# Query and key norms of eight attention heads, in two layouts: channel by token, and token by channel group

## The chip, the core and the metric

The kernel runs on one core of a Trainium2 chip: TensorE (PE) multiplies, VectorE (DVE), ScalarE (ACT) and GpSimd (POOL) work elementwise, SyncE (SP) issues most transfers. The metric is the device time of one execution in microseconds.

## The reference

One inference step of a layer: 512 prompt frames and 64 sample frames, width 2048, all in fp32. Only the attention heads matter here:

```python
def rmsnorm(x, g):
    xf = x.astype(jnp.float32)
    y = xf * lax.rsqrt(jnp.mean(xf * xf, axis=-1, keepdims=True) + EPS) * g.astype(jnp.float32)
    return y.astype(x.dtype)
...
hn = rmsnorm(x, g_norm1)
proj = hn @ w_in
q, k, v, gb, gc, hc = jnp.split(proj, ...)
q = rmsnorm(q.reshape(B, T, N_HEADS, HEAD_DIM), g_q)
k = rmsnorm(k.reshape(B, T, N_HEADS, HEAD_DIM), g_k)
v = v.reshape(B, T, N_HEADS, HEAD_DIM)
o_attn = stick_breaking_blocks(q, k_all, v_all, P).reshape(B, T, ATTN_W)
```

q and k are normed per frame and head, over 128 channels; the normed keys are an output. `EPS` is 1e-6. A convolution branch, an output projection and a gated feed-forward follow.

## The kernel before, in words

Data stands as channels on 128 partitions by 576 frames (512 and 64), in two halves of 288. Products of full precision take three PE matmuls in fp32r, with operands split into a high and a low part (`split`: a ScalarE copy makes the high part, a VectorE subtraction the low one). The weights of one projection of one head (2048 x 128) come in by SP, into one of two places of `raw_a`, and are split in two pieces of 1024 columns, by ScalarE (`whi`) and VectorE (`wlo`, once POOL).

The input's own row norm is not applied to x ahead of the projection; it is a factor per frame, R1, which `row_scale` spreads to all partitions with PE and by which the projections' results are multiplied.

The heads run one after the other. `head(h)` projects q, k and v (`project`: 2 halves of 16 channel blocks, 3 matmuls each); after each channel block the `Pipeline` ticks. Everything else of a head is a generator that sleeps for a number of ticks between its steps, so its matmuls stand at fixed places among the projections', and attention of head h runs while head h+1 projects. The order on PE is the order of the program; on ScalarE, VectorE and POOL a scheduler orders the instructions ahead of time, and each engine then takes them strictly in that order. SP's order is written out from head 1 on.

`norm_evac` (lines 619 to 644) handles q and k. When a half of the projection is done, VectorE multiplies it by R1 into `E`, ScalarE squares it, and the square is split. Some ticks later (13 for q, 16 for k) `rest` sums over channels with two matmuls with a matrix of ones (`channel_sums`, tile `ss`), which puts the sum on every partition; `rsqrt_mean` makes a reciprocal root from it, with logarithm, exponential and one Newton step, all 288 wide; then the result times gain is written as `qf` or `kf` and split into `qh`, `ql`, `kh`, `kl`. Behind k's second half `attend` is started, 15 ticks on (24 in head 0).

`attend` (660 to 781) computes scores z in three banks of PSUM from those parts, and scores `zs` against cached keys; softplus steps on ScalarE and VectorE; a mask of later queries as a POOL product with a 0/1 matrix `m01`; running sums as matmuls with triangular matrices (`trir`, `trif`); then `po`, the weighted values of the prompt (from `vtok` and its parts `vh`, `vl`), `cz` and `os` for the samples. `kb` is the transposed k in 32 x 32 blocks, made by VectorE from `kf`, which `put_tokens` stores.

In head 0 q is projected while x still comes in; its banks wait (`defer`) until k has been projected and `row_scale` has run, and q's and k's four halves follow, 4 ticks apart.

`x_sums` makes combinations of x for a later stage during the heads; its transfers, copies and subtractions (`o_ob`, `xs_out`) sit in the same queues.

Of the kernel before, what the change touches and what calls it, by code (L numbers as in the profile page):

```python
# [16 lines left out]
P = 128  # L17
# [77 lines left out]
def tile_hybrid_stream_step(  # L95
# [23 lines left out]
    lpad = ctx.enter_context(tc.tile_pool(name="lpad", bufs=1, side="left"))  # L119
    lpad.tile([P, 8], F32, name="lpad_t")  # L120
    rpad = ctx.enter_context(tc.tile_pool(name="rpad", bufs=1, side="right"))
    rpad.tile([P, 56], F32, name="rpad_t")
    acon = tc.alloc_tile_pool(name="acon", bufs=1, side="left")
    xt_dram = tc.dram_tile([KD, P, T], F32, name="xt_dram")
    x2_dram = tc.dram_tile([KD, P, T], F32, name="x2_dram")
# [95 lines left out]
    def split(hi, lo, src, lo_eng=None):  # L221
        nc.scalar.copy(out=hi, in_=src)  # L222
        (lo_eng or nc.vector).tensor_tensor(out=lo, in0=src, in1=hi.bitcast(F32), op=ALU.subtract)  # L223

    def parts(name):
        t = tmp.tile([P, 2, HALF], F32R, tag="hl", name=name)
        return t[:, 0], t[:, 1]
# [15 lines left out]
                            pattern=[[-1, P]], channel_multiplier=1)  # L243
    trir = acon.tile([P, P], F32R, name="trir")
    nc.vector.tensor_copy(trir, trif)
    m01 = acA[:, 3, :]
    nc.gpsimd.affine_select(out=m01, in_=onef, compare_op=ALU.is_ge, fill=0.0, base=-1,
                            pattern=[[1, P]], channel_multiplier=-1)
    mneg = acA[:, 4, :]
    nc.vector.tensor_scalar(out=mneg, in0=m01, scalar1=-NEG, scalar2=NEG, op0=ALU.mult, op1=ALU.add)  # L250
    s01 = acA[:, 5, :TS]
    nc.gpsimd.affine_select(out=s01, in_=onef[:, :TS], compare_op=ALU.is_ge, fill=0.0, base=TS - 1,
                            pattern=[[1, TS]], channel_multiplier=-1)
    nc.gpsimd.memset(s01[:TS, :], 0.0)
    sneg = acA[:, 5, TS:]
    nc.vector.tensor_scalar(out=sneg, in0=s01, scalar1=-NEG, scalar2=NEG, op0=ALU.mult, op1=ALU.add)

    ps_z = tc.alloc_tile_pool(name="ps_z", bufs=1, space=PSUM)

    def misc(name):  # L260
        return ps_z.tile([P, 512], F32, tag="misc", name=name, bufs=2)
# [3 lines left out]
    def load_vectors():  # L265
        r0 = 0
        for name, ap, n in (("gq", g_q[0], 1), ("gk", g_k[0], 1),
                            ("ga", g_attn_out[0], NH), ("gc", g_conv_out[0], NG),
                            ("cw", conv_w[0].rearrange("w d -> (w d)"), 3 * NG),
                            ("st", state_conv[0, 0].rearrange("w d -> (w d)"), 2 * NG), ("g2", g_norm2[0], KD)):  # L270
            rows[name] = r0
            nc.sync.dma_start(out=vraw[r0 : r0 + n, :], in_=ap.rearrange("(r c) -> r c", c=P))
            r0 += n

    g1c = const.tile([P, KD], F32, name="g1c")
    vec = const.tile([P, P], F32, name="vec")
# [12 lines left out]
    def col(name, i=0):  # L289
        return vec[:, rows[name] + i : rows[name] + i + 1]  # L290
# [177 lines left out]
    def channel_sums(src_hi, src_lo, a, b, name):  # L468
        ps = misc(name)[:, : b - a]
        mm(ps, oner, src_hi, start=True, stop=False)  # L470
        mm(ps, oner, src_lo, start=False, stop=True)
        return ps
# [13 lines left out]
                                op0=ALU.mult)  # L486
    split_weight(nc.vector)

    def project(evac, banks=(None, None), defer=None, then=None):
        whi, wlo = next_weight()  # L490
        if then:
            then()
        for bank, (a, b) in zip(banks, HALVES):
            if bank:
                ps = ps_z.tile([P, 512], F32, tag=bank, name="pjz")[:, :HALF]
            else:
                ps = ps_pj.tile([P, HALF], F32, tag="pj", name="pj")
            product(ps, whi, wlo, slice(0, P), x_two, KD, a // HALF)
            if defer is None:
                evac(ps, a, b)  # L500
            else:
                defer.append((evac, ps, a, b))

    def add_squares(acc, src, first):
        if first:
# [108 lines left out]

    free_places = []

    lags = [0]

    def norm_evac(name, gcol, dst_f, dst_hi, dst_lo, first, after=None):
        E = t1.tile([P, T], F32, tag="E", name=f"E{name}", bufs=2)  # L620

        def rest(a, b, sh, sl):
            if first:
                lags[0] += 4
            yield 6 + lags[0] if first else 16 if after else 13
            ss = channel_sums(sh, sl, a, b, "ss")
            r = tmp.tile([P, HALF], F32, tag="r", name="r")
            rsqrt_mean(r, ss, P, HALF)
            nc.vector.scalar_tensor_tensor(out=dst_f[:, a:b], in0=E[:, a:b], scalar=gcol, in1=r,
                                           op0=ALU.mult, op1=ALU.mult)  # L630
# [12 lines left out]

        return evac

    def put_tokens(t, dst, a, b):

# [12 lines left out]
    def attend(h, st):  # L660
# [49 lines left out]
        nc.vector.transpose(out=kb, in_=kf)  # L710
        yield 8
        put_tokens(kb, kp[:, h, :], 0, TP)
        put_tokens(kb, ks[:, h, :], TP, T)

# [90 lines left out]
    def head(h):  # L805
        st = {}
        st["cK"] = t1.tile([P, TP], F32, tag="cK", name="cK")
        st["cV"] = t1.tile([P, 4, P], F32, tag="cV", name="cV", bufs=2)
        for q in range(4):
            nc.sync.dma_start(out=st["cK"][32 * q : 32 * (q + 1), :].rearrange("t (b c) -> t b c", c=32),  # L810
                              in_=ck[:, h, 32 * q : 32 * (q + 1)].rearrange("(b t) c -> t b c", t=32))
        nc.sync.dma_start(out=st["cV"], in_=cv[:, h, :].rearrange("(i p) d -> p i d", p=P))
        for n in ("q", "k"):
            st[n + "f"] = t1.tile([P, T], F32, tag=n + "f", name=n + "f")
            st[n + "h"] = t1.tile([P, TP], F32R, tag=n + "h", name=n + "h")
            st[n + "l"] = t1.tile([P, TP], F32R, tag=n + "l", name=n + "l")
        q_evac = norm_evac("q", gqs, st["qf"], st["qh"], st["ql"], h == 0)
        k_evac = norm_evac("k", col("gk"), st["kf"], st["kh"], st["kl"], h == 0, after=attend(h, st))
        pipe.spawn(keys_cached(st, 20 if h else 59))
        if h == 0:  # L820
            waiting = [(q_evac, ps, a, b) for ps, (a, b) in zip(q0ps, HALVES)]
            project(k_evac, (None, "z1"), waiting)
            row_scale()
            for evac, ps, a, b in waiting:
                evac(ps, a, b)
# [1039 lines left out]
```

## Time and profile before

| what | us |
|---|---|
| runs, median (lowest to highest of 3) | 2370.59 (2369.72 to 2371.94) |
| the profiled execution | 2369.07 |
| its span | 2367.0 |
| three steady heads, 165.77 to 309.15 | 143.38 |
| of it PE busy | 143.38 |
| of it VectorE busy | 110.93 |
| of it ScalarE busy | 88.78 |
| of it POOL busy | 20.45 |

In the timeline, each row has the start, the length, the engine, the line, the operation, output and inputs, and the shape; in brackets how long the engine sat idle ahead of it and what ended that. Matmuls overlap in the pipeline: a projection matmul is shown as some 0.29 us long, but the next one starts 0.13 us after it. What a matmul costs PE is the distance from start to start. A matmul in plain fp32 stands as two records, one per pass.

In the view by stretches, a row has the stretch, its length, and for PE, the weight loads, VectorE, ScalarE and POOL the busy time with the number of instructions, then the granted clock of PE, the busy share of the DMA engines and GB/s. In the list of waits a row has the waiting instruction, what it waited for, the total, the number of times and the longest.

### The profile page before, as it was taken

Reading aid. Unit: us, or ns where it says so; the run is one execution under the profiler, and the core shown is the slowest. Engines: PE = TensorE matmul, PEld = TensorE weight load, DVE = VectorE, ACT = ScalarE, POOL = GpSimd, SP = SyncE. Lnnn points to the kernel's source line nnn. Section 1 sums busy time; section 2 is a strip of 40 time slices with the busy share of each in tenths; the row PEclk is TensorE's granted clock in tenths of the full one; section 3 lists DMA queues with packets and bytes.
Section 4 is the critical chain, followed back from the end, with each engine's and each line's share of the span. In section 5 each row is a group of like instructions: output and inputs, shape, how many; then the busy total and the mean of one; then the engine's idle time right before and its main releaser. Section 6 shows DMA issues by size and latency. Waiting matters only on the chain.

```text
span 2367.0 us, 43888 instructions
## 1 busy us (share of the span) xinstructions
PE 2340.9 (99%) x17581; PEld 2329.5 (98%) x17581; DVE 1935.3 (82%) x2908; ACT 1156.0 (49%) x2039; POOL 294.5 (12%) x386
## 2 busy tenths in 40 slices
PE   8999999999999999999999999999999999999998
PEld 8999999999999999999999999999999999999998
DVE  7878777788887889888888888888888777887896
ACT  6656655444444555444444444444444444444443
POOL 1011111341111230000000000000000002431221
PEclk9999999999999999999999999999999999999999
DMA  8466544684368654444444444444444936885553
GB/s 259 128 175 169 139 138 112 217 266 126 110 226 227 194 166 154 137 152 136 139 152 135 140 152 134 141 152 133 142 152 132 356 115 208 221 235 199 190 143 85
DMA packets 588804, 395.74 MB, mean 167 GB/s; under 512 B 100030, under 2 KB 577720, under 8 KB 588600
## 3 DMA queue, kind: packets, MB, share of 16 engines
q1 hardware_dynamic: 574776, 375.93, 50.9%
q0 software_dynamic: 8624, 16.22, 3.4%
q8 instruction: 137, 2.24, 0.4%
q10 hardware_dynamic: 5200, 0.79, 0.2%
q14 instruction: 67, 0.55, 0.1%
HBM read 301.45 MB, written 91.44 MB: 166 GB/s over the span
## 4 chain that ended last, share of the span: by engine, by line
PE 89%; DVE 5%; DMA 2%; ACT 2%; issue 1%; POOL 0%; ACTq 0%; SPq 0%; POOLq 0%; DVEq 0%
PE psy L1532 33%; PE psw L1532 16%; PE pj L213 13%; PE psx L1532 8%; PE psy L1036 6%; PE pjo L213 4%; PE psw L1036 3%; PE psx L1036 2%; DVE whl L223 1%; DMA raw_a<-in_w_down_dram 1%; PE po L747 1%; PE z L679 1%; ACT whl L222 0%; PE os L777 0%; DVE whl L1008 0%
## 5 line engine op out<-in xcount | busy, mean ns | idle before, releaser
L1532 PE MATMUL psy<-h_s,whl 128*128 128x288 f32 x2787 | 411.7, 294 | 1.7 <-ACT part L1542 1.7
L213 PE MATMUL pj<-x,whi 128*128 128x288 f32 x1856 | 390.5, 297 | 0.3 <-DVE x L356 0.3
L1532 PEld LDWEIGHTS psy<-h_s,whl 128*128 128x128 f32 x2787 | 383.5, 188 | 2.6 <-ACT part L1542 2.6
L223 DVE TENSOR_TENSOR whl<-raw_a,whl 128x1024 fp32r<-128x1024 f32 (+4 forms) x296 | 318.3, 1076 | 57.3 <-ACT whl L222 55.6
L1532 PE MATMUL psw<-t,whl 128*128 128x288 f32 x2400 | 346.9, 294 | 0.0
L1532 PEld LDWEIGHTS psw<-t,whl 128*128 128x128 f32 x2400 | 327.6, 188 | 0.0
L222 ACT CAST whl<-raw_a 128x1024 fp32r<-128x1024 f32 (+4 forms) x296 | 267.6, 906 | 116.7 <-issue 35.3
L213 PEld LDWEIGHTS pj<-x,whi 128*128 128x128 f32 x1856 | 305.0, 189 | 1.0 <-DVE x L356 0.6
L213 PE MATMUL pj<-x,wlo 128*128 128x288 f32 x928 | 274.5, 296 | 0.1
L223 DVE TENSOR_TENSOR whl<-raw_b,whl 128x1024 fp32r<-128x1024 f32 (+5 forms) x190 | 198.1, 1042 | 68.6 <-ACT whl L222 67.2
L222 ACT CAST whl<-raw_b 128x1024 fp32r<-128x1024 f32 (+5 forms) x190 | 164.9, 871 | 169.6 <-issue 73.1
L1542 ACT COPY part<-psy 128x288 f32<-128x288 f32 x242 | 96.7, 400 | 281.9 <-PE psy L1532 258.4
L1532 PE MATMUL psy<-t2t,whl 128*128 128x288 f32 x1212 | 183.5, 295 | 1.2 <-ACT part L1542 1.2
L1532 PE MATMUL psy<-b22m,whl 128*128 128x288 f32 x1212 | 183.1, 295 | 0.6 <-ACT part L1542 0.6
L213 PEld LDWEIGHTS pj<-x,wlo 128*128 128x128 f32 x928 | 174.9, 188 | 0.7 <-DVE wlo L423 0.3
L1532 PE MATMUL psx<-h_s,whl 128*128 128x288 f32 x1185 | 173.7, 294 | 0.0
L1532 PEld LDWEIGHTS psy<-t2t,whl 128*128 128x128 f32 x1212 | 168.3, 188 | 1.6 <-ACT part L1542 1.4
L1532 PEld LDWEIGHTS psy<-b22m,whl 128*128 128x128 f32 x1212 | 168.1, 188 | 0.9 <-ACT part L1542 0.9
L1532 PEld LDWEIGHTS psx<-h_s,whl 128*128 128x128 f32 x1185 | 162.7, 188 | 0.0
L222 ACT CAST whl<-s 128x1024 fp32r<-128x1024 f32 (+5 forms) x81 | 72.2, 892 | 101.7 <-PE psw L1532 99.4
L1311 POOL DMA_DIRECT2D hid_dram<-form x3 | 2.3, 751 | 947.2 <-DVE form L223 947.2
L1532 PE MATMUL psy<-t,whl 128*128 128x288 f32 x576 | 106.5, 294 | 0.0
(456 smaller groups left out, 4392.5 us busy)
## 6 DMA issues: line engine op xcount, KB each, us to landing
hid_dram<-form SPq DMA_DIRECT2D x147, 288.0 KB, 2.3
raw_a<-in_w_in_dram SPq DMA_DIRECT2D x41, 1024.0 KB, 6.1
raw_a<-in_w_gate_dram SPq DMA_DIRECT2D x22, 1024.0 KB, 6.1
raw_a<-in_w_up_dram SPq DMA_DIRECT2D x22, 1024.0 KB, 5.9
raw_b<-in_w_gate_dram SPq DMA_DIRECT2D x22, 1024.0 KB, 6.7
raw_b<-in_w_up_dram SPq DMA_DIRECT2D x22, 1024.0 KB, 7.0
h_s<-hid_dram SPq DMA_DIRECT2D x10, 2016.0 KB, 12.2
raw_a<-in_w_out_dram SPq DMA_DIRECT2D x16, 1024.0 KB, 5.5
```

The source lines that it names most:

```text
L213: mm(ps, w_[:, k, csl], x_, start=(k == 0 and n == 0), stop=(k == nk - 1 and n == 2))
L222: nc.scalar.copy(out=hi, in_=src)
L223: (lo_eng or nc.vector).tensor_tensor(out=lo, in0=src, in1=hi.bitcast(F32), op=ALU.subtract)
L679: mm(zb[i], a_[:, kk], b_[:, q0:TP], start=(n == 0), stop=False, skip_group_check=True)
L747: mm(po[:, i * P : 512], a_[:, i, :], b_[:, : 512 - i * P], stop=(i == 0 and n == 2), **kw)
L1036: mm(ps, whl[:, w_, j, :], x_, start=(start and j == 0 and q == 0), stop=(j == m - 1 and q == 2), skip_group_check=True)
L1311: q.dma_start(out=hid_dram[fp][2 * n - 2 : 2 * n].rearrange("f p t -> p f t"), in_=t.bitcast(F32))
L1532: mm(ps, whl[:, w_, j, :], x_, start=(start and j == 0 and q == 0), stop=(j == len(xs_) - 1 and q == 2), skip_group_check=True)
L1542: nc.scalar.copy(out=t, in_=st["y"])
```

## The change

A half of the projection is turned on arrival: VectorE transposes it in blocks of 32 x 32 straight out of PSUM into `E`. A partition then holds one frame out of each block of 32 and 32 channels of it; R1 is not multiplied in. ScalarE squares, and VectorE sums groups of 32, so that 18 columns of sums are left for a whole head's 576 frames. Once both halves are there, one matmul in plain fp32 with a 0/1 matrix `same` (partitions that agree modulo 32) adds the four channel groups. The reciprocal root is computed 18 columns wide; instead of EPS it adds EPS / R1 squared (`eps_r`, made once in `row_scale` from a turned R1). Then E is multiplied by it over all 576 columns, transposed back into `qf` or `kf`, scaled by the gain per channel on ScalarE, and split, for k in 384 columns only. k's token copy `kb` is no longer transposed from `kf`: POOL multiplies the normed E by the gain `gk_t`, which four small loads put on the partitions.

In head 0, q's banks are emptied ahead of k's projection; q's `rest` comes 38 ticks after, k's 8. The mask `m01` is gone: POOL selects in place (`later_queries`); `mneg` and `same` are made by POOL at the start.

```diff
-    rpad.tile([P, 56], F32, name="rpad_t")
+    small = rpad.tile([P, 56], F32, name="rpad_t")
+    NB = T // 32
+    eps_r, gk_t = small[:, :NB], small[:, NB : NB + 32]
...
-    m01 = acA[:, 3, :]
-    nc.gpsimd.affine_select(out=m01, in_=onef, compare_op=ALU.is_ge, fill=0.0, base=-1,
+    mneg = acA[:, 4, :]
+    nc.gpsimd.memset(mneg, 0.0)
+    nc.gpsimd.affine_select(out=mneg, in_=mneg, compare_op=ALU.is_ge, fill=NEG, base=-1,
                             pattern=[[1, P]], channel_multiplier=-1)
-    mneg = acA[:, 4, :]
-    nc.vector.tensor_scalar(out=mneg, in0=m01, scalar1=-NEG, scalar2=NEG, op0=ALU.mult, op1=ALU.add)
...
+    same = acA[:, 3, :]
+    nc.gpsimd.memset(same, 0.0)
+    for d in range(-3, 4):
+        nc.gpsimd.affine_select(out=same, in_=same, compare_op=ALU.not_equal, fill=1.0, base=32 * d,
+                                pattern=[[-1, P]], channel_multiplier=1)
...
+        for q in range(4):
+            nc.sync.dma_start(out=gk_t[32 * q : 32 * (q + 1), :],
+                              in_=g_k[0, 32 * q : 32 * (q + 1)].partition_broadcast(32))
...
         nc.vector.tensor_copy(R1[:, TP:], psr2[:, :TS])
+        turned = tmp.tile([P, T], F32, tag="hl", name="turned")
+        nc.vector.transpose(out=turned, in_=R1)
+        first = turned.rearrange("p (b c) -> p b c", c=32)[:, :, 0]
+        nc.vector.tensor_tensor(out=eps_r, in0=first, in1=first, op=ALU.mult)
+        nc.vector.reciprocal(out=eps_r, in_=eps_r)
+        nc.vector.tensor_scalar(out=eps_r, in0=eps_r, scalar1=EPS, scalar2=None, op0=ALU.mult)
...
-    def norm_evac(name, gcol, dst_f, dst_hi, dst_lo, first, after=None):
+    def norm_evac(name, gcol, dst_f, dst_hi, dst_lo, lag, kb=None, after=None):
         E = t1.tile([P, T], F32, tag="E", name=f"E{name}", bufs=2)
-
-        def rest(a, b, sh, sl):
-            if first:
-                lags[0] += 4
-            yield 6 + lags[0] if first else 16 if after else 13
-            ss = channel_sums(sh, sl, a, b, "ss")
-            r = tmp.tile([P, HALF], F32, tag="r", name="r")
-            rsqrt_mean(r, ss, P, HALF)
-            nc.vector.scalar_tensor_tensor(out=dst_f[:, a:b], in0=E[:, a:b], scalar=gcol, in1=r,
-                                           op0=ALU.mult, op1=ALU.mult)
-            e = min(b, TP)
-            split(dst_hi[:, a:e], dst_lo[:, a:e], dst_f[:, a:e])
-            if after and b == T:
+        Eb = E.rearrange("p (b c) -> p b c", c=32)
+        sq = tmp.tile([P, T], F32, tag="hl", name="sq")
+        sums = tmp.tile([P, HALF], F32, tag="sq", name="sums")[:, :NB]
+
+        def rest():
+            yield lag
+            ss = misc("ss")[:, :NB]
+            mm(ss, same, sums, start=True, stop=True)
+            ms, t = (tmp.tile([P, HALF], F32, tag=tag, name=tag, bufs=1)[:, :NB] for tag in ("ms", "t"))
+            y, r = (tmp.tile([P, HALF], F32, tag=tag, name=tag)[:, :NB] for tag in ("y", "r"))
+            stt = nc.vector.scalar_tensor_tensor
+            stt(out=ms, in0=ss, scalar=1.0 / P, in1=eps_r, op0=ALU.mult, op1=ALU.add)
+            nc.scalar.activation(out=y, in_=ms, func=AF.Ln)
+            nc.scalar.activation(out=y, in_=y, func=AF.Exp, scale=-0.5)
+            stt(out=t, in0=y, scalar=-0.5, in1=y, op0=ALU.mult, op1=ALU.mult)
+            nc.vector.tensor_tensor(out=t, in0=t, in1=ms, op=ALU.mult)
+            stt(out=r, in0=t, scalar=1.5, in1=y, op0=ALU.add, op1=ALU.mult)
+            nc.vector.tensor_tensor(out=Eb, in0=Eb, in1=r.unsqueeze(2).to_broadcast([P, NB, 32]), op=ALU.mult)
+            if kb is not None:
+                nc.gpsimd.tensor_tensor(out=kb.rearrange("p (b c) -> p b c", c=32), in0=Eb,
+                                        in1=gk_t.unsqueeze(1).to_broadcast([P, NB, 32]), op=ALU.mult)
+            nc.vector.transpose(out=dst_f, in_=E)
+            nc.scalar.activation(out=dst_f, in_=dst_f, func=AF.Copy, scale=gcol)
+            e = 3 * P if after else TP
+            split(dst_hi[:, :e], dst_lo[:, :e], dst_f[:, :e])
+            if after:
                 pipe.spawn(after)
 
         def evac(ps, a, b):
-            nc.vector.tensor_tensor(out=E[:, a:b], in0=ps, in1=R1[:, a:b], op=ALU.mult)
-            sq = tmp.tile([P, HALF], F32, tag="sq", name="sq")
-            sh, sl = parts("sq")
-            nc.scalar.activation(out=sq, in_=E[:, a:b], func=AF.Square)
-            split(sh, sl, sq)
-            pipe.spawn(rest(a, b, sh, sl))
+            nc.vector.transpose(out=E[:, a:b], in_=ps)
+            nc.scalar.activation(out=sq[:, a:b], in_=E[:, a:b], func=AF.Square)
+            nc.vector.reduce_sum(out=sums[:, a // 32 : b // 32], in_=sq[:, a:b].rearrange("p (b c) -> p b c", c=32),
+                                 axis=mybir.AxisListType.X)
+            if b == T:
+                pipe.spawn(rest())
...
+    def later_queries(t, base):
+
+        nc.gpsimd.affine_select(out=t, in_=t, compare_op=ALU.is_ge, fill=0.0, base=base,
+                                pattern=[[1, t.shape[1]]], channel_multiplier=-1)
...
-                nc.gpsimd.tensor_tensor(out=pb[i][:, :P], in0=pb[i][:, :P], in1=m01, op=ALU.mult)
+                later_queries(pb[i][:, :P], -1)
...
         yield 2
-        kb = t1.tile([P, T], F32, tag="kb", name="kb")
-        nc.vector.transpose(out=kb, in_=kf)
         yield 8
+        kb = st["kb"]
...
-        q_evac = norm_evac("q", gqs, st["qf"], st["qh"], st["ql"], h == 0)
-        k_evac = norm_evac("k", col("gk"), st["kf"], st["kh"], st["kl"], h == 0, after=attend(h, st))
+        st["kb"] = t1.tile([P, T], F32, tag="kb", name="kb")
+        q_evac = norm_evac("q", gqs, st["qf"], st["qh"], st["ql"], 13 if h else 38)
+        k_evac = norm_evac("k", col("gk"), st["kf"], st["kh"], st["kl"], 16 if h else 8, st["kb"], attend(h, st))
         pipe.spawn(keys_cached(st, 20 if h else 59))
         if h == 0:
-            waiting = [(q_evac, ps, a, b) for ps, (a, b) in zip(q0ps, HALVES)]
-            project(k_evac, (None, "z1"), waiting)
+            for ps, (a, b) in zip(q0ps, HALVES):
+                q_evac(ps, a, b)
+            project(k_evac, (None, "z1"))
             row_scale()
-            for evac, ps, a, b in waiting:
-                evac(ps, a, b)
```

More of the change, by code (lines that the diff above doesn't have):

```diff
@@ L487, in tile_hybrid_stream_step, with project @@
     split_weight(nc.vector)
-    def project(evac, banks=(None, None), defer=None, then=None):
+    def project(evac, banks=(None, None), then=None):
         whi, wlo = next_weight()
@@ L498, in project @@
             product(ps, whi, wlo, slice(0, P), x_two, KD, a // HALF)
-            if defer is None:
-                evac(ps, a, b)
-            else:
-                defer.append((evac, ps, a, b))
+            evac(ps, a, b)
     def add_squares(acc, src, first):
@@ L615, in tile_hybrid_stream_step @@
     free_places = []
-    lags = [0]
-    def norm_evac(name, gcol, dst_f, dst_hi, dst_lo, first, after=None):
+    def norm_evac(name, gcol, dst_f, dst_hi, dst_lo, lag, kb=None, after=None):
         E = t1.tile([P, T], F32, tag="E", name=f"E{name}", bufs=2)
-        def rest(a, b, sh, sl):
-            if first:
-                lags[0] += 4
-            yield 6 + lags[0] if first else 16 if after else 13
-            ss = channel_sums(sh, sl, a, b, "ss")
-            r = tmp.tile([P, HALF], F32, tag="r", name="r")
-            rsqrt_mean(r, ss, P, HALF)
-            nc.vector.scalar_tensor_tensor(out=dst_f[:, a:b], in0=E[:, a:b], scalar=gcol, in1=r,
-                                           op0=ALU.mult, op1=ALU.mult)
-            e = min(b, TP)
-            split(dst_hi[:, a:e], dst_lo[:, a:e], dst_f[:, a:e])
-            if after and b == T:
+        Eb = E.rearrange("p (b c) -> p b c", c=32)
[23 more added lines that the diff above has]
+            if after:
@@ L816, in head @@
             st[n + "l"] = t1.tile([P, TP], F32R, tag=n + "l", name=n + "l")
-        q_evac = norm_evac("q", gqs, st["qf"], st["qh"], st["ql"], h == 0)
-        k_evac = norm_evac("k", col("gk"), st["kf"], st["kh"], st["kl"], h == 0, after=attend(h, st))
+        st["kb"] = t1.tile([P, T], F32, tag="kb", name="kb")
+        q_evac = norm_evac("q", gqs, st["qf"], st["qh"], st["ql"], 13 if h else 38)
+        k_evac = norm_evac("k", col("gk"), st["kf"], st["kh"], st["kl"], 16 if h else 8, st["kb"], attend(h, st))
         pipe.spawn(keys_cached(st, 20 if h else 59))
         if h == 0:
-            waiting = [(q_evac, ps, a, b) for ps, (a, b) in zip(q0ps, HALVES)]
-            project(k_evac, (None, "z1"), waiting)
+            for ps, (a, b) in zip(q0ps, HALVES):
+                q_evac(ps, a, b)
+            project(k_evac, (None, "z1"))
             row_scale()
-            for evac, ps, a, b in waiting:
-                evac(ps, a, b)
         else:
```

## The prediction

> **What bounds the kernel now.** I read the busy shares first, then the heads' own stretches, then what TensorE (PE) waited for, then the stretches where that happened.
>
> ```profile
> span 2367.0 us, 43888 instructions
> PE 2340.9 (99%) x17581; PEld 2329.5 (98%) x17581; DVE 1935.3 (82%) x2908; ACT 1156.0 (49%) x2039; POOL 294.5 (12%) x386
> 213.56:261.35 47.79, 47.79 (x358) 47.43 (x358) 38.89 (x74) 30.55 (x65) 6.59 (x14) 1.00 0.60 162
> ```
>
> The third line is one head out of the view by stretches: 47.79 us, in all of which PE is busy, at the full granted clock (1.00). So in a steady head every PE instruction counts at its start-to-start spacing, and VectorE and ScalarE count only where PE waits for them. The waits of PE in the heads:
>
> ```profile
> PE z L679 <- ACT kh L222: 2.0, 1, 2.0
> PE ss L470 <- ACT sq L222: 0.4, 1, 0.4
> PE ss L470 <- DVE ms L461: 0.3, 1, 0.3
> PE ss L471 <- DVE sq L223: 0.2, 1, 0.2
> ...
> 67.60 0.29 PE L213 MATMUL pj<-x,whi 128*128 128x288 f32 x1
> 69.92 0.38 PE L679 MATMUL z<-qh,kh 128*128 128x256 f32 x1 [2.03 <-ACT kh L222]
> 70.60 0.39 PE L679 MATMUL z<-qh,kl 128*128 128x256 f32 x1 [0.29 <-DVE kl L223]
> 70.82 0.28 PE L679 MATMUL z<-ql,kh 128*128 128x256 f32 x1
> ...
> 140.56 0.38 PE L744 MATMUL po<-pr,vtok 128*128 128x128 f32 x2
> 141.18 0.39 PE L747 MATMUL po<-ph,vh 128*128 128x256 f32 x1 [0.23 <-ACT vh L222]
> 142.20 0.38 PE L747 MATMUL po<-ph,vl 128*128 128x256 f32 x1 [0.63 <-DVE vl L223]
> 142.42 0.28 PE L747 MATMUL po<-pl,vh 128*128 128x256 f32 x1
> ```
>
> Four come from the list of waits, the rest from the timeline. By starts: z should have come 0.13 after 67.60 and the next two 0.12 apart, so it lost 2.19 + 0.56 + 0.10 = 2.85 us, where the waits add to 2.3. The same way po (head 1's values, run during head 2) lost 0.40 + 0.90 + 0.10 = 1.40 for 0.8. The ss waits of 0.9 I count as 1.5 in that proportion. In all 5.8 us are lost.
>
> **The change, part by part.**
>
> *Matmuls removed.* Each head sums squares over channels with 8 matmuls of 288 columns (q and k, two halves, high and low part).
>
> ```profile
> 251.08 0.29 PE L471 MATMUL ss<-sq,oner 128*128 128x288 f32 x1
> 251.21 0.30 PE L213 MATMUL pj<-x,whi 128*128 128x288 f32 x1
> 253.98 1.05 PE L777 MATMUL os<-ws,cV 128*128 128x128 f32 x8
> 254.87 0.39 PE L777 MATMUL os<-ws,vtok 128*128 128x128 f32 x2
> 258.27 0.28 PE L679 MATMUL z<-qh,kh 128*128 128x256 f32 x1
> ...
> 18.91 0.71 PE L333 MATMUL psx_s<-ident,xsn 64*128 64x64 f32 x8
> 19.55 0.66 PE L339 MATMUL psx<-ident,xin 128*128 128x128 f32 x4
> ```
>
> From ss to the next start is 0.13: 64 x 0.131 = **8.4 us** off PE, all of it on the path.
>
> *Matmuls added.* 16 of 18 columns in plain fp32, each two passes (the four os matmuls stand as x8). A pass of 128 columns takes 0.89/8 = 0.111, one of 64 columns 0.64/8 = 0.080. By columns alone 18 would take 0.02; the dearest I allow is 0.111 per pass plus a break of 0.10 as behind kl. So one matmul costs 0.04 to 0.32. I take 0.18, near the 64-column row: **+2.9 us** (0.7 to 5.1). [...]
>
> *The path of k, heads 1 to 7.* Now one chain per head lies between the ss matmul of k and the scores z, and its order on VectorE is unbroken in the built program, apart from x-sum work in a few heads. Its prices:
>
> ```profile
> 39.83 0.17 DVE L439 TENSOR_SCALAR ssr<-ssr 128x5 f32<-128x5 f32 x1
> 253.64 0.75 DVE L223 TENSOR_TENSOR xs_out<-o_ob,xs_out 128x576 fp32r<-128x576 f32 x1
> 256.76 0.78 DVE L710 STREAM_TRANSPOSE kb<-kf 128x576 f32<-128x576 f32 x1
> 232.27 0.55 DVE L223 TENSOR_TENSOR pl<-pr,ph 128x384 fp32r<-128x384 f32 x1
> 28.68 0.21 ACT L348 COPY st<-psx_s 128x64 f32<-128x64 f32 x1
> 30.48 0.78 ACT L353 ACTIVATE x<-st,g1c 128x576 fp32r<-128x576 f32 x1
> 230.74 0.51 ACT L222 CAST ph<-pr 128x384 fp32r<-128x384 f32 x1
> ```
>
> Matmul to first VectorE step 0.35 (a little over the 0.29 of the ss row), ms 0.2, logarithm and exponential 0.25 each, three small steps 0.6, the product 0.8, the transpose 0.83, the scale copy 0.83, kh 0.55, kl 0.55: 5.2 us. PE has work for 258.27 - 251.21 = 7.1 us there. Slack 1.9, cost nothing; without that cover each us would cost 7. Before, the late half's chain ended just ahead of z too. VectorE loses 16 steps of about 0.45 for q and k per head and the kb transpose; it gains four PSUM transposes, four group sums, eight small steps and six wide ones. Of a transpose out of PSUM there is no row; at 0.45 (as other 288-wide steps) to 0.9 it sits behind a projection with three banks to rotate, hence nothing.
>
> *POOL.* The mask becomes a select, and k's token copy kb becomes a POOL product.
>
> ```profile
> 1.34 0.29 POOL L242 TENSOR_SCALAR_AFFINE_SELECT acA<-acA 128x128 f32<-128x128 f32 x1
> 246.97 0.84 POOL L510 TENSOR_TENSOR acc_a<-acc_a,sqm 128x288 f32<-128x288 f32 x1 [6.19 <-ACT sqm L509]
> 50.80 4.97 POOL L176 TENSOR_TENSOR wlo<-raw_a,whi 128x1024 fp32r<-128x1024 f32 x2 [9.51 <-ACT whi L175]
> 49.68 1.05 ACT L175 CAST whi<-raw_a 128x1024 fp32r<-128x1024 f32 x1
> 41.32 0.60 SPq L183 DMA_DIRECT2D raw_a<-in_w_in_dram  x1
> raw_a<-in_w_in_dram SPq DMA_DIRECT2D x41, 1024.0 KB, 6.1
> 47.34 0.40 PE L213 MATMUL pjz<-x,whi 128*128 128x288 f32 x1
> 53.72 2.37 DVE L464 TENSOR_TENSOR t<-y 128x288 f32<-128x288 f32 x1 [0.20 <-ACT y L463]
> 254.73 0.45 DVE L464 TENSOR_TENSOR t<-y 128x288 f32<-128x288 f32 x1
> ```
>
> A select of 0.29 is no dearer than the product it replaces, and kb, twice the 0.84, ends 1.7 us after k's product, before kl and before the store, which comes 10 ticks behind z. Nine more POOL steps at the start, 2.5 us, end before POOL's first weight split; the four small loads of g_k stand behind the vector loads, while SP waits for a weight slot. Both at nothing.
>
> *Head 0.* Attention there comes 14 ticks earlier. The rows show a price: t took 2.37 (others of its line 0.45) and ended when POOL's two weight splits (50.80 + 4.97) had ended. [...] The weight of those splits, issued at 41.32, lands 6.1 later, and one cast of 1.05 on, at 48.5, POOL starts, until 53.5: k's squares no longer hold the casts up. The eps row (a product, a reciprocal, a scale) is due on VectorE from 49.1 and meets both splits. Then: q's ms 53.8, its r 55.0, product 56.0, transpose 57.0; k's r 57.8 behind Ev, product 58.65; kcT, ql and kf's transpose to 60.75; copy 61.55, kh 62.1, kl 62.65. PE (99 projection matmuls of 0.132 and two ss from 47.34) is at z by 60.75. It waits 1.35 + 0.4 + 0.1 = **+1.9 us** (0 if the lock isn't met, 3.5 if the load of that weight lands 1.5 later).
>
> *Head 1.* In the built order, head 0's vh and vl stand behind q's whole chain (scale copy, qh, ql); before, vh ran in time:
>
> ```profile
> 84.87 0.51 ACT L222 CAST vh<-vtok 128x384 fp32r<-128x384 f32 x1
> 131.50 1.22 DVE L176 TENSOR_TENSOR wlo<-raw_a,whi 128x1024 fp32r<-128x1024 f32 x1
> ```
>
> Counted from q's ss: ms, held by two splits of pl, ends at 1.05; the exponential, between sp's steps, 1.95; k's square 2.9; the group sum 3.55; r 3.7; product 4.5; transpose 5.3; copy 6.1; qh 6.75; vh 7.3; vl 8.05. PE gets to po's second matmul after 27 matmuls and two more, 4.0. Lost 3.3 + 0.65 + 0.1: **+4.0 us**. Without the sp and square steps the chain is 2 us shorter (2.0 at least); with a 1.22 split held up behind it, 4.6. In the later heads vh stands ahead of the chain, and po's old 1.40 is gone.
>
> *Elsewhere*: in head 4 both queues have an x-sum step that waits for a DMA ahead of k's chain; +0.4 (0 to 2.5).
>
> **Sum:** -8.4 + 2.9 - 5.8 + 1.9 + 4.0 + 0.4 = -5.0 us. The profiled execution took 2369.07 (span 2367.0 and 2.1 around it): 2364.1. The runs' median is 1.5 above it, so **2365.6 us**. [...]
>
> **Rivals.**
> 1. *The waits eat it.* Gain stays 5.5 on the matmuls, but head 0 loses 3.0, head 1 4.6 and some x-sum heads 1.5: -2.2, 2368.4. [...] 0.22.
> 2. *Slower: k late in every head.* If kf's transpose were held by kb as t was by wlo, the chain is 5.2 + 1.7 = 6.9, still under 7.1. It decides from 8.5 us a chain (1.4 x 7 = 9.8 eats 5.0 and passes 0.2%); at 8.8, with logarithm and exponential at full 288 price and three x-sum steps of 0.5 in between, +11.9 - 5.0: 2377. Against: the slack of 1.9, and those steps stand there in few heads. 0.07. No row here tests a transpose that starts under a long POOL step. [...]
> 3. *Head 0 and 1 go smoothly* (no lock met, po waits 2.0): -5.0 - 1.9 - 2.0 = -8.9, 2361.7. 0.17.
> 4. *It doesn't do what it says*: the matmuls were hidden anyway. The fully busy 47.79 speaks against it; 2370.6 then, 0.01.
>
> **How the numbers follow.** My case, -3.3 to -7, has 0.53; rivals 1 to 4 have 0.22, 0.07, 0.17 and 0.01. About 0.2% (4.7 us, so below 2365.9) is what a measurement of this kernel tells from no change; of my case, centred at -5.0, 0.33 lies beyond it and 0.20 within. Faster 0.33 + 0.17 = 0.50, same 0.20 + 0.22 + 0.01 = 0.43, slower 0.07. All good ends together give -11.5, all bad ones +1.5; they won't all fall one way, and eight in ten I put at 2361 to 2370.2.
>
> **What would show it.** A steady head of 47.1 instead of 47.79. ss start to next start of 0.16 to 0.22. No PE wait at z in heads 1 to 7; one at head 0's z of about 2; none at ss; one at po around 115 us, vh then vl, about 4, and none in head 2. Wrong: heads at 47.8 or longer (then ss is dearer or k's chain late), or no wait at head 1's po.

## The result, and the profile after

| kernel | median us (lowest to highest, runs) | against before, 95 % interval |
|---|---|---|
| before | 2370.74 (2368.18 to 2374.89, 20) | |
| after | 2367.25 (2363.19 to 2370.51, 20) | 0.9983 (0.9977 to 0.9989) |

The change makes the kernel 0.17 % faster, 3.5 us. The profiled execution of after took 2369.78, span 2368.1, so it is one of its slower ones; why that matters is shown below.

First the page of after and one steady head (from one first z matmul to the next; the columns are those of the prediction's row of 47.79):

```profile
span 2368.1 us, 43722 instructions
...
211.36:258.56 47.20, 47.20 (x354) 46.84 (x353) 33.28 (x63) 27.97 (x56) 7.88 (x15) 1.00 0.60 167
```

A head takes 47.20 instead of 47.79, PE is still busy in all of it, and VectorE has lost 5.6 us of work per head. All heads from the second on have this period. The price of the new sum matmul stands in the timeline of after:

```profile
234.58 0.29 PE L215 MATMUL pj<-x,whi 128*128 128x288 f32 x1
234.71 0.29 PE L639 MATMUL ss<-sums,acA 128*128 128x18 f32 x2
234.85 0.38 PE L215 MATMUL pj<-x,whi 128*128 128x288 f32 x1
235.07 0.30 PE L215 MATMUL pj<-x,wlo 128*128 128x288 f32 x1
```

Its two passes take 0.138 from start to start, but the projection matmul behind it takes 0.22 to its next start instead of 0.13. The whole price is 0.138 + 0.084 = 0.222.

The list of waits of after, as far as it answers to the lines of before:

```profile
PE z L708 <- ACT kh L224: 2.8, 1, 2.8
PE po L775 <- ACT vh L224: 2.2, 1, 2.2
...
PE psy L1064 <- ACT part L1073: 1.3, 2, 0.7
```

In the heads only two waits are left, each once and with a short one of 0.20 behind it (in brackets in the next rows): head 0's z, and po of head 0's values, which runs during head 1. The waits of psy come later, ahead of the output projection. None at ss, none at z in heads 1 to 7, none at po in head 2. By starts, in PE's timeline:

```profile
59.25 0.29 PE L215 MATMUL pj<-x,whi 128*128 128x288 f32 x1
62.29 0.39 PE L708 MATMUL z<-qh,kh 128*128 128x256 f32 x1 [2.75 <-ACT kh L224]
62.88 0.58 PE L708 MATMUL z<-qh,kl 128*128 128x256 f32 x1 [0.20 <-DVE kl L225]
...
91.15 0.38 PE L772 MATMUL po<-pr,vtok 128*128 128x128 f32 x2
93.75 0.58 PE L775 MATMUL po<-ph,vh 128*128 128x256 f32 x1 [2.22 <-ACT vh L224]
94.54 0.58 PE L775 MATMUL po<-ph,vl 128*128 128x256 f32 x1 [0.20 <-DVE vl L225]
...
97.37 0.44 PE L215 MATMUL pj<-x,whi 128*128 128x288 f32 x1
97.61 0.44 PE L215 MATMUL pj<-x,wlo 128*128 128x288 f32 x1
```

z lost 2.91 + 0.47 + 0.1 = 3.5 (without a wait the next start is 0.13 behind the first row and 0.12 behind the second). po lost 2.46 + 0.58 + 0.1 = 3.1 (0.14 and 0.21 without a wait, in the rows of a version below). And there is something that none of the rows of before shows: the last two rows are ordinary projection matmuls, 0.24 apart instead of 0.13. In the next rows the stretches are cut where the granted clock of PE, the third number from the end, changes, and the first of each pair holds the wait:

```profile
59.46:62.87 3.41, 0.47 (x2) 0.19 (x1) 2.03 (x4) 1.92 (x3) 0.19 (x1) 1.00 0.48 77
62.87:66.29 3.42, 3.41 (x11) 3.12 (x12) 3.35 (x4) 2.94 (x6) 0.00 (x0) 0.50 1.16 337
...
90.18:93.59 3.41, 1.35 (x11) 1.16 (x9) 1.86 (x3) 1.69 (x3) 1.57 (x4) 1.00 0.01 2
93.59:100.42 6.83, 6.46 (x22) 5.88 (x23) 1.65 (x3) 1.71 (x4) 0.00 (x0) 0.50 0.01 2
```

Behind each of the two waits PE ran at half clock (0.50), for 3.41 us and for 6.83 us. Half of the work done in that time is the price: 3.41 x 0.50 = 1.7 behind z and 6.46 x 0.50 = 3.2 behind po, not much less than the waits themselves.

How the parts add up shows in the distance from the last matmul of `row_scale` to the first z of head 7, in before, in after, and, to be used below, in the version with both waits removed and in before with its own waits at z and po removed:

```profile
46.98 0.43 PE L450 MATMUL ps_r1s<-dg,acA 64*128 64x64 f32 x2
...
401.65 0.28 PE L679 MATMUL z<-qh,kh 128*128 128x256 f32 x1
```

```profile
45.34 0.43 PE L460 MATMUL ps_r1s<-dg,acA 64*128 64x64 f32 x2
...
400.16 0.28 PE L708 MATMUL z<-qh,kh 128*128 128x256 f32 x1
```

```profile
48.09 0.43 PE L460 MATMUL ps_r1s<-dg,acA 64*128 64x64 f32 x2
...
392.12 0.28 PE L708 MATMUL z<-qh,kh 128*128 128x256 f32 x1
```

```profile
45.64 0.43 PE L450 MATMUL ps_r1s<-dg,acA 64*128 64x64 f32 x2
...
395.13 0.28 PE L679 MATMUL z<-qh,kh 128*128 128x256 f32 x1
```

The distances are 354.67, 354.82, 344.03 and 349.49 us. (The first rows differ by up to 2.8 us; in that is PE's wait for a load of x at psx, in the lists of waits 0.7 us in before, 1.6 in the version with both waits removed and none in the other two.) In these two executions the heads are no shorter at all after the change: what its matmuls and vanished waits gain, 10.6, the two new waits and the half clock behind them take back. The four parts above add up to 11.5 and the distances give 10.8 (354.82 - 344.03), so a part is counted twice: behind po the half clock began at 93.59, before the waits there were over.

Why the waits are there is seen on the other engines. Head 0, POOL and VectorE in the timeline of after:

```profile
50.30 4.75 POOL L178 TENSOR_TENSOR wlo<-raw_a,whi 128x1024 fp32r<-128x1024 f32 x2 [10.62 <-ACT whi L177]
58.42 1.23 POOL L651 TENSOR_TENSOR kb<-Ek,rpad_t 128x576 f32<-128x576 f32 x1 [3.38 <-DVE Ek L649]
```

```profile
51.57 1.16 DVE L646 SCALAR_TENSOR_TENSOR t<-y 128x18 f32<-128x18 f32 x1 [2.48 <-ACT y L645]
52.76 2.32 DVE L647 TENSOR_TENSOR t<-t,ms 128x18 f32<-128x18 f32 x1
...
58.88 1.32 DVE L225 TENSOR_TENSOR ql<-qf,qh 128x512 fp32r<-128x512 f32 x1
```

The two 18-wide steps t of q end where POOL's first and second weight split end (52.7 and 55.05). Together they took 3.5 us, where two such steps take 0.36 in a steady head, and k's chain stands behind q's. The subtraction ql, 0.69 in the other heads, took 1.32 beside POOL's kb (58.42 to 59.65) and held up kf's transpose.

Head 1, ScalarE:

```profile
91.86 0.77 ACT L654 ACTIVATE qf<-qf,gqs 128x576 f32<-128x576 f32 x1 [2.32 <-DVE qf L653]
92.67 0.62 ACT L224 CAST qh<-qf 128x512 fp32r<-128x512 f32 x1
93.19 0.51 ACT L224 CAST vh<-vtok 128x384 fp32r<-128x384 f32 x1
```

ScalarE stands idle for 2.32 us until q's transpose has run, while vh waits behind.

In a steady head k's chain has room (PE, VectorE and POOL of after, in order of time):

```profile
204.04 0.29 PE L639 MATMUL ss<-sums,acA 128*128 128x18 f32 x2
206.52 0.78 DVE L653 STREAM_TRANSPOSE kf<-Ek 128x576 f32<-128x576 f32 x1
206.56 1.22 POOL L651 TENSOR_TENSOR kb<-Ek,rpad_t 128x576 f32<-128x576 f32 x1 [9.24 <-DVE Ek L649]
208.68 0.56 DVE L225 TENSOR_TENSOR kl<-kf,kh 128x384 fp32r<-128x384 f32 x1 [1.39 <-ACT kh L224]
```

From ss to the end of kl 5.2 us pass; z is due at 211.36.

### The profile page after: what moved, and what is told of

It is laid out like the page before. It is cut to its first block, busy times and chain, and to the rows that moved or that the text cites. A ratio compares the mean times of both kernels' runs of the same rounds, so it can differ in the third digit from the quotient of the medians.

```text
span 2368.1 us, 43722 instructions
## 1 busy us (share of the span) xinstructions
PE 2340.6 (99%) x17549; PEld 2329.2 (98%) x17549; DVE 1897.4 (80%) x2823; ACT 1134.2 (48%) x1975; POOL 302.3 (13%) x403
## 4 chain that ended last, share of the span: by engine, by line
PE 88%; DVE 5%; DMA 3%; ACT 2%; issue 1%; ACTq 0%; POOL 0%; SPq 0%; POOLq 0%; DVEq 0%
PE psy L1560 33%; PE psw L1560 16%; PE pj L215 13%; PE psx L1560 8%; PE psy L1064 6%; PE pjo L215 4%; PE psw L1064 3%; PE psx L1064 1%; DVE whl L225 1%; DMA raw_a<-in_w_out_dram 1%; PE z L708 1%; PE po L775 1%; DMA raw_b<-in_w_down_dram 1%; DMA out_dram<-acc 1%; ACT whl L224 0%
```

## The experiments

Three answers to "where did the gain go" stood against each other: the two waits alone; the waits and the half clock behind them; and a loss further on, since the first matmul of the output projection starts at the same time before and after, although head 7's z had come 1.49 earlier:

```profile
781.81 0.29 PE L213 MATMUL pjo<-mixm,whi 128*128 128x288 f32 x1
```

```profile
781.83 0.29 PE L215 MATMUL pjo<-mixm,whi 128*128 128x288 f32 x1
```

| version | median us (runs) | mean granted clock of the runs | against before |
|---|---|---|---|
| after | 2367.25 (20) | 0.9978 | 0.9983 |
| z later | 2362.79 (5) | 0.9986 | 0.9962 (0.9948 to 0.9975) |
| po later | 2361.22 (5) | 0.9988 | 0.9955 (0.9943 to 0.9968) |
| z and po later | 2359.35 (5) | 0.9992 | 0.9945 (0.9932 to 0.9957) |
| z later, q's chain of head 1 later | 2357.93 (5) | 0.9990 | 0.9945 (0.9932 to 0.9957) |
| before, z and po later | 2363.74 (6) | 0.9995 | 0.9971 (0.9959 to 0.9982) |

The kernel before, run beside them, had a mean clock of 0.9989 to 0.9992. A thousandth of clock is 2.4 us, but only roughly: the mean takes in the end of an execution, where PE has nothing left to do. In the profiled execution of z and po later half clock begins at 2354.15 for the first time, and PE's last matmul started at 2352.17.

**z later** (the changed kernel, only head 0's scores moved):

```diff
-        yield 15 + (9 if h == 0 else 0)
+        yield 15 + (18 if h == 0 else 0)
...
-        yield 18
+        yield 9 if h == 0 else 18
         mm(zb[3], trif, pb[3], stop=False, **kw)
```

> The changed kernel with head 0's scores z nine ticks (3.6 us) later and the sleep behind them nine ticks shorter, so that only z moves. My theory (each wait costs its own length): no wait for kh at head 0's z, 2.91 + 0.47 + 0.1 = 3.5 us less, 2363.8 in the median against 2367.25. Rival one (behind a wait of over 2 us PE goes on at half clock, which costs as much again): besides those 3.5 us the half clock from 62.3 to 66.5 goes, 1.7 us more, so -5.2 and 2362; the granted clock is 1.00 in that stretch. Rival two (what the heads gain is given back in the stage at 735 to 785 us, where weights come late): the heads end 3.5 to 5 us earlier, but the first pjo still starts near 781.8, and the time stays at 2366 to 2367.

Measured 2362.79, 4.5 less. The wait at z is gone; that at po is still there, 3.4 by starts, with half clock behind it from 92.19 to 95.61. More than the wait's own 3.5 went and less than the 5.2 of the profiled execution, presumably because not every run has the half clock. The output projection now starts at 777.05, 4.8 earlier: it isn't held at 781.8.

**po later**:

```diff
-        yield 16
+        yield 25 if h == 0 else 16
         vtok, vh, vl = st["vtok"], st["vh"], st["vl"]
...
-        yield 18
+        yield 13 if h == 0 else 18
         cz = misc("cz")
...
-        yield 16
+        yield 12 if h == 0 else 16
         os_ = misc("os")
```

> The changed kernel with head 0's po nine ticks later and the two sleeps behind it five and four ticks shorter. My theory: no wait for vh and vl at po in head 1, 2.38 + 0.67 + 0.1 = 3.1 us less, 2364.1. Rival one (half clock behind the wait): the stretch from 93.7 to 100.2 us at 0.50 goes too, 3.3 us more, so -6.4 where the clock drops in a run; in the median, in which a part of the runs drop, 2361.5 to 2363. Rival two (given back at 735 to 785): pjo still starts near 781.8, time 2366 to 2367.

Measured 2361.22, 6.0 less: twice the 3.1 of the wait. Here the wait at z, with everything ahead of it unchanged, was 1.78 + 0.47 instead of 2.91 + 0.47, and no half clock followed it. In this execution PE had waited 1.7 us for a load of x at psx, which after has not (the last matmul of `row_scale` at 48.05, not 45.34), and so PE came later to the same weights.

**z and po later**, both edits:

> Both edits together. My theory: the waits alone, 3.5 + 3.1 = 6.6 us less than the changed kernel, 2360.7. Rival one (half clock behind them): another 1.7 + 3.3 us against the profiled execution of the changed kernel, 2357 to 2359 in the median, and a mean granted clock of 0.999 or 1.0 instead of 0.997 to 0.998. Rival two (given back at 735 to 785): heads end 7 to 12 us earlier, pjo starts near 781.8 all the same, 2366.

Measured 2359.35, 7.9 less than after. The stretch in which both waits stood, in this version's view by stretches:

```profile
60.00:100.00 40.00, 40.00 (x299) 39.63 (x298) 29.28 (x52) 24.78 (x48) 5.66 (x13) 1.00 0.57 153
```

PE is busy throughout at full clock. Waits alone would have given 2360.7; the mean clock rose from 0.9978 to 0.9992, worth some 3.3 us, and both together 2357.4. The median lies between, so the time alone doesn't part these two answers; that the half clock went with the waits is read from the row. The output projection:

```profile
774.14 0.29 PE L215 MATMUL pjo<-mixm,whi 128*128 128x288 f32 x1
```

It starts 7.7 earlier than in after, where head 7's z came 8.0 earlier. So the third answer falls: nothing pins that stage. What it does take back is small: from head 7's z to this matmul pass 380.16 in before, 381.67 in after, 382.02 in this version and 382.11 in before with z and po later (its first pjo starts at 777.24). In after this is the two waits of psy for part in the list above, 0.8 each by starts, which before had only once, as 0.16. What is late there wasn't tried.

**Weight split on VectorE**:

```diff
-            split_weight(nc.gpsimd if i == 2 else nc.vector)
+            split_weight(nc.vector)
```

> The changed kernel with the first weight split of the heads on VectorE instead of POOL. If POOL's split holds up the 18-wide steps of q's chain in head 0 (my theory), the two t steps that took 1.16 and 2.32 us take 0.15 to 0.2 each, as in the other heads. If something else made them long (their own inputs, a read out of another bank), they stay over 1 us. The wait at z is no clean measure here, since VectorE takes up 2.4 us of splits; 1 to 3 us of it stay.

The same two steps in its timeline:

```profile
54.15 0.18 DVE L646 SCALAR_TENSOR_TENSOR t<-y 128x18 f32<-128x18 f32 x1 [0.54 <-ACT y L645]
54.37 0.18 DVE L647 TENSOR_TENSOR t<-t,ms 128x18 f32<-128x18 f32 x1
```

0.18 each: POOL's split made them long. ql, still under POOL's kb here, still took 1.19. z's waits were 1.31 and 1.52, since a split now stands ahead of kl, and half clock followed them. In this version the order on ScalarE had changed in head 1 as well: vh ran at 89.69, ahead of qf's copy at 92.56, and po didn't wait. The time, 2364.07 in one run, is therefore no measure of the weight split alone.

**q's chain behind vh** (z later, and besides):

```diff
-        q_evac = norm_evac("q", gqs, st["qf"], st["qh"], st["ql"], 13 if h else 38)
+        q_evac = norm_evac("q", gqs, st["qf"], st["qh"], st["ql"], 13 + 10 * (h == 1) if h else 38)
```

> The version with z of head 0 later (2362.79, po wait 2.78 + 0.66 us and half clock from 90.4 to 95.5 us), and now head 1's q chain ten ticks later, so that on ScalarE and VectorE vh and vl of head 0 stand ahead of the whole chain; po itself stays where it is. If vh was late only because it stood behind that chain (my theory): vh runs behind the last sp step, some 1.5 us ahead of po, the wait at po goes, with it the half clock, and the time is that of the version with z and po later, 2357 to 2360. If vh was late because its own data came late (the load of vtok) or because ScalarE was simply full there: the wait at po stays over 2 us, 2362 to 2363, and the q chain, now later, may add a wait at head 1's z.

In the timeline of that version, ScalarE and then PE:

```profile
86.32 0.50 ACT L224 CAST vh<-vtok 128x384 fp32r<-128x384 f32 x1
```

```profile
87.36 0.38 PE L772 MATMUL po<-pr,vtok 128*128 128x128 f32 x2
87.50 0.36 PE L775 MATMUL po<-ph,vh 128*128 128x256 f32 x1
87.71 0.28 PE L775 MATMUL po<-ph,vl 128*128 128x256 f32 x1
```

vh runs ahead of po and neither z nor po waits. Its data had been there; only its place in the queue made it late. 2357.93 is the fastest version of the study (it can't be told from z and po later): 0.9945 against before, where the change as it came has 0.9983.

**The sum matmul twice** (z and po later, and a second one that nobody reads):

```diff
             mm(ss, same, sums, start=True, stop=True)
+            pipe.spawn(again(sums), 1)
...
+    def again(sums):
+        mm(misc("ss2")[:, :NB], same, sums, start=True, stop=True)
+        yield 1
```

> The version with z and po later, with every one of the 16 new sum matmuls issued a second time one channel block later (the second result is not used): a price measured alone, read from the steady head of 47.20 us, which has two of them. By the two passes alone (0.027 + 0.111 = 0.138 us from start to start) it becomes 47.48. By my 0.18 it becomes 47.56. By 0.222, which counts the 0.084 us by which the projection matmul behind each of them is longer (0.216 to its next start instead of 0.132), it becomes 47.64. By the dearest price allowed, 0.32, 47.84.

A steady head of that version:

```profile
202.78:250.42 47.64, 47.64 (x358) 47.28 (x357) 33.29 (x63) 27.95 (x56) 7.87 (x15) 1.00 0.61 167
```

Against 47.20, two more make 0.44: 0.22 each. The longer matmul behind belongs to the price.

**Waits put in** (z and po later; in three kernels n is 1, 5 and 11):

```diff
+    def stall():
+        yield 64
+        few = small[:, 50:56]
+        s1 = misc("s1")[:, :6]
+        mm(s1, same, eps_r[:, :6], start=True, stop=True)
+        nc.scalar.copy(out=few, in_=s1)
+        for _ in range(n):
+            nc.scalar.activation(out=few, in_=few, func=AF.Copy)
+        mm(misc("s2")[:, :6], same, few, start=True, stop=True)
...
+        if 0 < h < 7:
+            pipe.spawn(stall())
```

> The version with z and po later (median 2359.35, mean granted clock 0.9992), with a wait put into each of heads 1 to 6: a small matmul, a chain of six small ScalarE steps from its result, and a second matmul on what they give; by 0.24 us a step and some 0.4 of handing over PE stands still for about 1.9 us. If a wait costs its own length only, each adds 1.9 to 2.2 us, 12 to 13 in all, and the granted clock stays at 0.999. If every wait over about 1.5 us brings the half clock, some 3 us more for each, 30 in all, and a mean clock near 0.992. If it depends on the length and on chance, as the 1.5 to 2 us waits at 890 us suggest (half clock behind two of six), 1 to 3 of the 6 are followed by it: 15 to 22 us.

> The same with eleven steps instead of five behind the first copy, about 3.3 us of standing still in each of heads 1 to 6. If a wait costs its own length only: 20 to 21 us in all, 2380, and the granted clock as before. If waits of 2.8 us and more always bring the half clock (four of four so far): behind each of the six some 3 to 6 us at 0.50, which costs half of that, 9 to 20 us in all on top, 2389 to 2400, and a mean clock of 0.992 to 0.996.

> The version with z and po later, with the same wait in each of heads 1 to 6 as in the two runs before it, but only two ScalarE steps long. There, six steps became waits of 2.2 to 4.3 us, and all twelve waits were followed by half clock. Two steps should make waits of 1 to 3 us, by what else stands in ScalarE's queue. If half clock needs 2.8 us or more, none or few of the six are followed by it, the mean clock stays at 0.998 to 0.999, and the time is 2359.35 and the waits themselves, 2366 to 2375. If length hardly matters, all six are: a clock of 0.993 to 0.995 and 2380 or more. If chance decides between 1.5 and 2.8 us, some are, and two waits of the same length differ.

ScalarE's own work stood between the steps, so the waits came out longer than planned, by starts:

| n | six waits, us | followed by half clock | mean clock | median us |
|---|---|---|---|---|
| 1 | 1.27, 2.64, 2.35, 2.35, 3.35, 2.87 | all but the 1.27 | 0.9947 | 2383.77 |
| 5 | 2.23, 3.60, 3.74, 3.30, 4.30, 3.83 | all | 0.9920 | 2396.22 |
| 11 | 5.85, 5.44, 5.18, 4.74, 5.74, 5.27 | all | 0.9903 | 2404.21 |

The shortest and a longer one of n = 1, in PE's timeline, and the clock in the stretches behind the two:

```profile
94.61 0.39 PE L638 MATMUL s<-rpad_t,acA 128*128 128x6 f32 x2 [1.13 <-ACT rpad_t L637]
...
196.46 0.39 PE L638 MATMUL s<-rpad_t,acA 128*128 128x6 f32 x2 [2.20 <-ACT rpad_t L637]
```

```profile
94.70:97.70 3.00, 3.00 (x23) 3.00 (x24) 2.18 (x2) 2.31 (x3) 0.00 (x0) 1.00 0.00 0
...
196.50:200.50 4.00, 4.00 (x20) 4.00 (x21) 1.75 (x2) 0.47 (x1) 0.00 (x0) 0.60 0.22 35
```

With n = 5 the waits add to 21.0; the median is 36.9 over the version without them. The rest, 15.9 or 2.6 for each wait, goes to the half clock and the small matmuls put in (the mean clock alone, 0.9920 instead of 0.9992, would be some 17). "Needs 2.8 us or more" falls: 2.23 was enough. It went not by the length but by where the wait lay, as the last section shows.

**Before, z and po later**:

```diff
-        yield 15 + (9 if h == 0 else 0)
+        yield 15 + (17 if h == 0 else 0)
...
-        yield 18
+        yield 10 if h == 0 else 18
...
-        yield 16
+        yield 20 if h == 1 else 16
...
-        yield 18
+        yield 16 if h == 1 else 18
...
-        yield 16
+        yield 14 if h == 1 else 16
```

> The kernel before the change, with head 0's z eight ticks later and head 1's po four ticks later, and the sleeps behind them shorter by as much. My theory counts 2.85 us for its wait at z and 1.40 for that at po: 4.2 less, 2366.5. If these waits weren't on the path that sets the end, or turn up elsewhere: 2370.7 as before. If half clock follows them in some runs of the kernel before as well, up to 2 us more gain: 2364.5. Against the changed kernel with both waits removed (2359.35) the rest is what the sums by groups of 32 bring by themselves: about 64 x 0.131 less 16 x 0.222, 4.8 us, and the ss waits, 1 to 1.5.

Measured 2363.74, against 2371.62 of before beside it. One short wait at ss is left (0.5 in the list of waits). Steady heads stay at 47.79. The distance to head 7's z fell from 354.67 to 349.49, by 5.2: 1.4 of it at po, as counted, and 3.8 around z, where 2.85 were counted. The rest of the median's 7.9 isn't all explained; the mean clock, 0.9989 beside 0.9995, is worth 1.4. This version of the old kernel has a lower median than the changed one as it came (2367.25), though the two intervals against before overlap a little. With both freed of their waits at z and po, the change itself is worth 344.03 - 349.49 = -5.5 in the heads, and 4.4 in the medians (3.6 if each is set against the runs of before beside it).

## Why the prediction was right, and where it was off

Forecast 2365.6, measured 2367.25, on the side that was forecast. That it came so near is in part luck. Some 3 us of half clock, which the sum didn't have, went off the gain; without them it would have been 6 to 7 us, not the 5.0 of the sum. Of what made up for them, 0.9 is the cheaper wait in head 1 and 0.4 the x-sum heads; the rest isn't accounted for. Its own steps:

- *Removed matmuls, 8.4, and the view that PE counts start to start*: right. The distance in the heads bears out this term, the added matmuls and the old waits taken together: -8.4 + 16 x 0.222 - 5.8 is -10.65, and from before to the version without waits it is 344.03 - 354.67 = -10.64. The single parts fit less closely.
- *Added matmuls, 0.18 each, 2.9*: mis-sized. 0.222 each, 3.55. The prediction took the passes by a row of other matmuls and left out that the next projection matmul pays too.
- *Old waits, 5.8, on the path*: right. In before with z and po later 5.2 went, where 4.25 had been counted for these two; the 1.5 for ss was not measured by itself.
- *k's path with a slack of 1.9 in heads 1 to 7*: right; 5.2 us as estimated, z 2.1 behind it. The second rival falls: the transpose kf starts as POOL's kb does (206.52 and 206.56) and still takes 0.78. The prediction found no row of a transpose that starts under a POOL step; before has one far behind the heads, at 2309.22, 0.36 into a POOL step of 1.10, and it takes 0.76. A transpose out of PSUM took 0.48, the low end of the 0.45 to 0.9.
- *Head 0, +1.9*: mechanism right, place and size off. Not the eps row met the splits (it was done by 48.2, before POOL began) but the two steps t of q, and ql then met kb: 3.5 in the profiled execution, 2.35 in another. What the prediction calls the lock, here and in its third rival, no run shows as such; measured is that a step t begun during POOL's split ended just behind it (0.32 us in before, 0.03 to 0.04 in after) and took 2.37 us instead of 0.45 in before, 1.16 and 2.32 instead of 0.18 in after, and 0.18 with that split on VectorE. The 3.5 is the upper end that was named, and its condition held: that weight's first cast started at 49.17, behind the transfer, where 47.4 had been reckoned.
- *Head 1, +4.0*: mechanism right, vh behind q's chain; 3.1 instead of 4.0, and at 91 to 95 us, not around 115.
- *Elsewhere, +0.4*: nothing in the heads; none from the third on has a PE wait. But some 1.5 us went in the stage ahead of the output projection, at the waits of psy, which the sum doesn't have.
- *Missing from the sum*: the half clock behind the two new waits, 1.7 and 3.2 in the profiled execution. No rival held it. In before a wait of 2.19 + 0.56 at z and one of 1.6 at 890 us had been followed by a clock of 1.00, and so a wait was priced at its own length. The mean clock of 0.9978 against 0.9989 to 0.9992 puts it at some 3 us in the mean run, more than the distance between forecast and result.

What isn't settled: the parts as the profiled execution of after shows them would make a smaller gain than the median's 3.5. That execution had its wait at z longer, by the earlier start, than the one of po later, and the lowest clock (0.997; the fastest run, 2363.19, has 1.000), so other runs probably meet cheaper waits; by how much each wasn't measured.

## What to carry to other kernels

In these heads, where PE is busy throughout, a wait on it cost its length and, where it left PE with 1.92 us of work or less in one step of 3.41 us, half clock behind it as well: 1.7 us for one step in after, 3.2 for two (next section). Price a wait by both, and look at the granted clock in the stretch after each wait before taking the sum. A change that shortens a chain also moves its steps among the queues and past other engines' long steps: here moving two generators by a few ticks brought more (7.9 us) than the change itself as it came (3.5). Before a layout change is credited, give the old kernel the same retiming.

## What the runs showed of the hardware

The granted clock of PE changed in steps of 3.41 us. In after it changed at 62.87, 66.29, 93.59, 100.42, 892.31 and 895.72, all whole multiples of 3.413 us apart, and within the work of all twelve traces a stretch at 0.50 lasted one such step or two, 3.41 or 6.83 us. It went by how long PE was busy in the step before, not by how long the wait was. The same wait of 1.63 us for the squares ahead of the gated stage, at 889.8 us, was followed by half clock in after and not in before, because it lay otherwise across the steps (views by stretches, first after, then before, whose steps are counted back from 2366.41, its one drop, after the last matmul; the second row of each goes on behind the wait):

```profile
888.90:892.31 3.41, 1.78 (x12) 1.33 (x11) 3.24 (x9) 1.53 (x4) 0.00 (x0) 1.00 0.35 67
891.00:897.00 6.00, 5.22 (x25) 5.01 (x26) 6.00 (x10) 2.49 (x5) 0.00 (x0) 0.72 0.94 296
```

```profile
888.44:891.86 3.42, 1.96 (x14) 1.64 (x12) 3.25 (x9) 1.53 (x4) 0.00 (x0) 1.00 0.25 63
891.00:897.00 6.00, 5.24 (x37) 5.03 (x38) 6.00 (x10) 3.29 (x6) 0.00 (x0) 1.00 0.90 301
```

With 1.78 us of PE work in the step, as this view counts it, the clock fell; with 1.96 it didn't. The other two drops within after's work stand behind steps with 0.47 (59.46 to 62.87) and 1.35 (90.18 to 93.59); before has none within its work, where the least in a step was 1.93 (495.91 to 499.32). Cut into such steps, the twelve traces give some 8200 at full clock. In 40 of them PE was busy for 1.92 us or less, and half clock followed 39 (the other is in the last microseconds of an execution); it followed none of those with 1.93 or more. At half clock, full clock came back behind a step in which PE was busy throughout (27 steps), and not behind one in which it was busy for 3.17 us or less (16 steps); in after it came back behind the steps from 62.87, 97.01 and 892.31, with 3.41 us each, and not behind the one from 93.59, with 3.05.

So the 17 longer waits that were put in, of 2.23 us and more, all brought half clock: each left one step with at most 1.59 us of work. The one of 1.27 left 2.28. The wait at z in before, 2.19 + 0.56, fell across two steps, with 2.07 and 2.44 us of work, and brought none. The 1.78 + 0.47 of po later left 1.93 and brought none either. The 1.31 and 1.52 of the version with the weight split on VectorE lay almost whole in one step, with 1.11, and did. Where the steps fell differed between executions (888.90 in after, 888.44 in before), and with it what the same wait cost.

An 18-wide VectorE step with two inputs (`t<-t,ms`) took 2.32 us instead of 0.18 while POOL split weights, and ql 1.32 instead of 0.69 beside POOL's product kb, where the transpose kf, begun as that product did, lost nothing (0.78).
